# A hybrid decoder layer: weight sums of the seven-product pieces formed in earlier stages, kept in device memory, and used in every second piece

## The chip, the cores and the metric

The kernel runs on one core of one Trainium2 chip. Its time is the device time of one execution in microseconds, and lower is better. Five engines work side by side, each through its own list of instructions in a fixed order: PE (TensorE, matrix products), DVE (VectorE), ACT (ScalarE), POOL (GpSimd) and SP (SyncE, which here only issues transfers). Transfers issued by SP, ACT and POOL run on the core's 16 DMA engines. An instruction that has to wait holds up all that stand behind it on its engine.

## The reference

One layer of a decoder with 256 tokens and 16 meta tokens in front, width 2048, all in float32. What costs time are four weight matrices:

```python
h    = concat([meta, x])                                   # 272 x 2048
proj = rms_norm(h) @ w_in                                  # 2048 -> 12320
yA   = grouped_rms_norm(B * conv3(C * v))                  # short convolution, 16 groups
yB   = grouped_rms_norm(SSD(silu(conv4(xBC)), dt) * silu(z))   # state space, 8 groups
h    = h + rms_norm(concat([yA, yB]) @ w_out)              # 4096 -> 2048
h    = h + rms_norm(square(relu(rms_norm(h) @ w_ff1)) @ w_ff2)  # 2048 -> 8192 -> 2048
return h[16:]
```

Weights have 4 bytes each: 100 MB for `w_in`, 34 MB for `w_out`, 67 MB each for `w_ff1` and `w_ff2`. All are read once from device memory.

## The kernel before

**Three products for one.** TensorE multiplies in a format with fewer bits (float32r), so each operand is split into a high part (a rounded copy, made by ACT) and a low part (the difference, made by DVE). A product is then high x high + high x low + low x high: three matmuls.

**Pieces.** The weights come in 256 pieces of 1 MB, each 128 partitions x 2048 values: 96 of `w_in`, 32 of `w_out`, 64 of `w_ff1`, 64 of `w_ff2`. For a piece, SP loads `raw` (three buffers), ACT makes `wh` (three buffers), DVE makes `wl` (two or three), PE uses both. `load(i)` writes this down; the program asks for a piece two ahead of the one that PE works on. A raw buffer is free for the next load once `wl` has been made from it.

**Stages.** (1) Input projection: 24 groups of four pieces; activations are the moving operand, so the results stand feature by feature, and the convolutions, the state-space part and the group norms of earlier groups are worked in between by DVE, ACT and small matmuls. The first four pieces are loaded in 16 slices of 128 rows (`split_input`), each with one slice of the input. (2) Output projection and (4) second feed-forward product: `tok_stationary`. Here tokens are stationary, in two blocks of 128, the weights move 512 columns at a time, and the output is done in two halves of 1024 columns; a piece has two slices of 128 rows and 1024 columns. (3) First feed-forward product, 16 blocks of four pieces.

**The seven-product form.** A plain piece of stage 2 or 4 is a 2 x 2 block product (two token blocks, two slices of rows, two column blocks): eight block products, 24 matmuls of 512 columns. In some pieces the Strassen-Winograd form is used: seven block products, 21 matmuls, for which four sums of weights (`t`, then its parts `th`, `tl`) and four sums of activations (`js`, then `mix`) are needed. Some of the products go into a second set of four PSUM banks, `shared`, which is spread over the outputs once in each half (`spread_shared`, `shared_late`). Before the change 5 pieces of `w_out` and 14 of `w_ff2` (every fourth) take this form. Their sums are made shortly before use by `add_up` (L189 to L194): DVE subtracts 128 x 1024 and twice 128 x 512, ACT copies, DVE subtracts 128 x 2048.

**What sets the order.** The instructions are written in program order and then ordered for each engine, at build time, by a scheduler with a timeline of its own (`schedule_with_timeline_sim=True`); an instruction may be put ahead of others when its engine and its inputs are free in that timeline. The order doesn't change when the kernel runs. `later` and `pump` place small matmuls between the large ones.

In the profile of the kernel before, L175 makes `wl` in the projection and L174 its `wh`; L646 to L648 and L643 are the projection's matmuls; L1089 and L1090 those of the first feed-forward product; L791 to L793 those of plain pieces in `tok_stationary`, L822 to L824 of seven-product pieces. In the changed kernel lines are some 13 to 34 higher.

Of the kernel before, what the change touches and what calls it, by code (L numbers as in the profile page):

```python
# [9 lines left out]
F32 = mybir.dt.float32  # L10
# [36 lines left out]
def hymba_layer(ctx: ExitStack, tc: tile.TileContext, ht, x, meta, vec, cst, g1, g3,  # L47
# [14 lines left out]
    raws = ctx.enter_context(tc.tile_pool(name="raws", bufs=3, side="right"))  # L62
    yctx = ctx.enter_context(ExitStack())
# [116 lines left out]
    seven, sums = {}, {}  # L180

    def add_up(i):

        if i not in seven or i in sums:
            return
        raw = fetch(i, ("raw",))[0]
        rows_in(i, raw, slice(0, 2))
        t, th, tl = seven[i]()
        nc.vector.tensor_sub(t[:, 0:2], raw[:, :, 512:], raw[:, 0].rearrange("p (a n) -> p a n", a=2))  # L189
        nc.vector.tensor_sub(t[:, 2], raw[:, 1, 512:], t[:, 0])  # L190
        nc.vector.tensor_sub(t[:, 3], raw[:, 1, :512], t[:, 2])
        for half in (slice(0, 2), slice(2, 4)):
            nc.scalar.copy(th[:, half], t[:, half])
        nc.vector.tensor_sub(tl, t, th)  # L194
        sums[i] = (raw, th, tl)

    def load(i):
# [34 lines left out]
    cst_sb = const.tile([P, NCST], F32, name="cst_sb")  # L232
# [69 lines left out]
    with ExitStack() as p1:  # L302
# [24 lines left out]

        def split_input(k):
# [9 lines left out]
            if k == 8:  # L338
                nc.sync.dma_start(vec_sb[:, V_GCN:], vec[:, V_GCN:])
                nc.sync.dma_start(cst_sb, cst)  # L340
# [139 lines left out]
        def dt_consts():  # L480
            ts(vec_sb[:, V_CW:V_DSK], vec_sb[:, V_CW:V_DSK], 0.5, None, op0=ALU.mult)
            nc.vector.tensor_copy(nsel.rearrange("p i m -> p (i m)"), cst_sb[:, C_NS:C_NS + 384])
# [5 lines left out]
        pers = p1.enter_context(tc.tile_pool(name="pers", bufs=1))  # L488
        xem, bmt = [], []
# [165 lines left out]
        for gi, (kind, idx) in enumerate(groups):  # L655
# [12 lines left out]
            for j in range(4):  # L668
# [9 lines left out]
                wh, wl = parts[4 * gi + j]  # L678
                if gi == 4:
# [69 lines left out]
    def tok_stationary(base, korder, src, parity, dst, gain, ssq, r, tail, done, between, late=None, sixth=None,  # L749
                       fast=((), ()), mixp=None, half_gain=None):  # L750
# [7 lines left out]
        for h in range(2):  # L758
            for i in fast[h]:
                seven[base + npc * h + i] = room  # L760

        def prep(i):
# [10 lines left out]
            if base + i in seven:  # L773
                a11, a21, a12, a22 = (s[:, k, P * b:P * (b + 1)] for k in range(2) for b in range(2))
                a = left.tile([P, 4, P], F32, tag="junk", name="js")
                ah_, al_ = mixes()
# [18 lines left out]
        def mixes():  # L795
# [3 lines left out]
        def seven_products(d, x, h, i, first, last):  # L799
# [15 lines left out]
            def t(j):  # L815
                return th[:, j], tl[:, j]
# [353 lines left out]
```

## Time and profile before

| | |
|---|---|
| time, median of 3 runs | 1507.97 us (1507.62 to 1508.58) |
| the profiled execution | 1508.04 us, of which the span from the first to the last instruction is 1506.2 us |
| PE | 1490.7 us busy, 9187 matmuls |
| DVE | 1117.2 us busy, 1680 instructions |
| ACT | 839.4 us busy, 1303 instructions |
| POOL | 1.1 us busy, 8 instructions |
| DMA | 281.49 MB, 187 GB/s over the span |
| HBM | 277.90 MB read, 2.10 MB written |

In a profile row an instruction is named by line, engine, operation, and what it writes and reads (`wl<-raw,wh`), then the sizes. In rows in order of time the first number is the start in us, the second the duration; `x2` means that instructions in a row were put together. In rows by groups the numbers behind the bar are busy time in us, the mean of one in ns, and the idle time of the engine before them with what ended it. In rows of stretches there is the busy time of each engine with its number of instructions, then the clock granted to TensorE, the share of time that the DMA engines were busy, and their GB/s.

### The profile page before, as it was taken

The page shows a single profiled execution, that of the slowest core. Times are in us where ns is not written, and L with a number is a line of the kernel's source. Part 1 is how long each engine was busy: PE and PEld are TensorE (multiplying, and loading weights), DVE is VectorE, ACT ScalarE, POOL GpSimd, SP SyncE. Part 2 cuts the span into 40 slices and gives each one's busy share as a digit, 9 for nine tenths or more (in the row PEclk, how much of TensorE's full clock was granted, in tenths as well). Part 3 has the DMA queues.
Part 4 walks back from the last instruction along what each step waited for, and adds up shares of the span by engine and source line. Part 5 has one row for each costly group of instructions (what it writes and reads, how often), then busy time and mean ns, then how long its engine had stood idle before and what let it go on. Part 6 is the DMA issues. An engine that isn't in the chain of part 4 may idle for free.

```text
span 1506.2 us, 23037 instructions
## 1 busy us (share of the span) xinstructions
PE 1490.7 (99%) x9187; PEld 1337.3 (89%) x9187; DVE 1117.2 (74%) x1680; ACT 839.4 (56%) x1303; POOL 1.1 (0%) x8
## 2 busy tenths in 40 slices
PE   8999999999999999999999999999999999999997
PEld 8999899999999999988887888888888888888886
DVE  7698888667765776797878666666666788789776
ACT  6655555455544554556557655556556555556552
POOL 0000000000000000000000000000000000000000
PEclk9999999999999999999999999999999999999999
DMA  9665555556545646575664555565555656657562
GB/s 306 230 191 159 150 143 166 163 173 169 167 144 185 176 149 215 188 232 196 197 222 143 193 186 184 190 196 192 184 188 191 210 196 208 209 161 247 190 201 84
DMA packets 151676, 281.49 MB, mean 187 GB/s; under 512 B 8064, under 2 KB 59392, under 8 KB 150912
## 3 DMA queue, kind: packets, MB, share of 16 engines
q1 hardware_dynamic: 150848, 275.83, 57.1%
q10 hardware_dynamic: 720, 4.19, 0.7%
q8 instruction: 72, 1.18, 0.3%
q14 instruction: 36, 0.29, 0.1%
HBM read 277.90 MB, written 2.10 MB: 186 GB/s over the span
## 4 chain that ended last, share of the span: by engine, by line
PE 95%; DMA 2%; DVE 1%; ACT 1%; issue 0%; SPq 0%; DVEq 0%; ACTq 0%
PE mm L1089 15%; PE mm L648 11%; PE mm L647 10%; PE mm L646 10%; PE mm L791 9%; PE mm L792 9%; PE mm L793 9%; PE mm L1090 7%; PE mm L643 3%; PE mm L823 2%; PE mm L824 2%; PE mm L822 2%; DMA raw<-w_in 2%; PE aux L613 1%; PE mm L1007 1%; PE mm L1005 1%
## 5 line engine op out<-in xcount | busy, mean ns | idle before, releaser
L648 PE MATMUL mm<-XX,wl 128*128 128x256 f32 (+3 forms) x1536 | 427.2, 285 | 0.0
L646 PE MATMUL mm<-XX,wh 128*128 128x258 f32 (+3 forms) x1344 | 382.1, 288 | 5.4 <-ACT wh L174 5.4
L647 PE MATMUL mm<-XX,wh 128*128 128x258 f32 (+3 forms) x1344 | 379.3, 286 | 0.0
L1089 PE MATMUL mm<-h,wh 128*128 128x512 f32 x960 | 333.2, 394 | 0.0
L175 DVE TENSOR_TENSOR wl<-raw,wh 128x1024 fp32r<-128x1024 f32 (+1 forms) x223 | 256.0, 1182 | 99.5 <-PE mm L648 56.5
L174 ACT CAST wh<-raw 128x1024 fp32r<-128x1024 f32 (+1 forms) x223 | 218.0, 1017 | 164.8 <-PE mm L647 121.9
L648 PEld LDWEIGHTS mm<-XX,wl 128*128 128x128 f32 x1536 | 286.5, 189 | 1.4 <-issue 0.2
L1090 PE MATMUL mm<-h,wl 128*128 128x256 f32 x960 | 265.7, 277 | 0.0
L646 PEld LDWEIGHTS mm<-XX,wh 128*128 128x128 f32 x1344 | 253.1, 190 | 7.7 <-ACT wh L174 5.4
L647 PEld LDWEIGHTS mm<-XX,wh 128*128 128x128 f32 x1344 | 252.6, 189 | 1.5 <-issue 0.7
L216 DVE SCALAR_TENSOR_TENSOR wl<-raw,vec_sb,wh 128x512 fp32r<-128x512 f32 x256 | 175.5, 747 | 98.5 <-ACT wh L215 98.5
L792 PE MATMUL mm<-wl,jh 128*128 128x512 f32 x616 | 239.4, 389 | 0.0
L793 PE MATMUL mm<-wh,jl 128*128 128x512 f32 x616 | 239.0, 389 | 0.0
L791 PE MATMUL mm<-wh,jh 128*128 128x512 f32 x616 | 233.1, 390 | 0.0
L1089 PEld LDWEIGHTS mm<-h,wh 128*128 128x128 f32 x960 | 180.0, 188 | 41.5
L222 DVE TENSOR_TENSOR wl<-raw,wh 128x2048 fp32r<-128x2048 f32 x75 | 171.8, 2290 | 56.0 <-ACT wh L220 53.4
L215 ACT ACTIVATE wh<-raw,vec_sb 128x512 fp32r<-128x512 f32 x256 | 163.8, 712 | 87.0 <-PE mm L1089 50.5
L1090 PEld LDWEIGHTS mm<-h,wl 128*128 128x128 f32 x960 | 180.3, 188 | 0.3
L220 ACT CAST wh<-raw 128x1024 fp32r<-128x1024 f32 x150 | 149.5, 1045 | 39.6 <-PE mm L824 25.5
L792 PEld LDWEIGHTS mm<-wl,jh 128*128 128x128 f32 x616 | 115.6, 188 | 23.9
L793 PEld LDWEIGHTS mm<-wh,jl 128*128 128x128 f32 x616 | 115.6, 188 | 23.9
L791 PEld LDWEIGHTS mm<-wh,jh 128*128 128x128 f32 x616 | 115.6, 188 | 24.0
(610 smaller groups left out, 1470.4 us busy)
## 6 DMA issues: line engine op xcount, KB each, us to landing
raw<-w_ff SPq DMA_DIRECT2D x128, 1024.0 KB, 5.1
raw<-w_in SPq DMA_DIRECT2D x60, 1024.0 KB, 5.2
raw<-w_out SPq DMA_DIRECT2D x32, 1024.0 KB, 5.1
raw<-w_in SPq DMA_DIRECT2D x80, 256.0 KB, 4.8
raw<-w_in SPq DMA_DIRECT2D x32, 512.0 KB, 4.1
xn<-x SPq DMA_DIRECT2D x2, 1024.0 KB, 5.2
xt<-x ACTq DMA_DIRECT2D x2, 1024.0 KB, 6.3
out<-fg SPq DMA_DIRECT2D x8, 256.0 KB, 2.1
```

Source lines behind the costliest of these rows:

```text
L174: nc.scalar.copy(wh[:, ks], raw[:, ks])
L175: nc.vector.tensor_sub(wl[:, ks], raw[:, ks], wh[:, ks])
L216: stt(wl[:, k], raw[:, k], g, wh[:, k].bitcast(F32), op0=ALU.mult, op1=ALU.subtract)
L222: nc.vector.tensor_sub(wl, raw, wh)
L646: mm(o[:, :n], lhsT=wh[:, k, fs], rhs=XH[kk][:, lo:], start=(kk == 0), stop=False)
L647: mm(o[:, :n], lhsT=wh[:, k, fs], rhs=XL[kk][:, lo:], start=False, stop=False)
L648: mm(o[:, :n], lhsT=wl[:, k, fs], rhs=XH[kk][:, lo:], start=False, stop=last)
L791: mm(o, lhsT=yh[:, k, bs], rhs=wh[:, k, ns], start=first, stop=False)
L792: mm(o, lhsT=yh[:, k, bs], rhs=wl[:, k, ns], start=False, stop=False)
L793: mm(o, lhsT=yl[:, k, bs], rhs=wh[:, k, ns], start=False, stop=last)
L1089: mm(o, lhsT=wh[:, k, fs], rhs=both, start=(kk == 0), stop=False)
L1090: mm(o[:, :SEQ], lhsT=wl[:, k, fs], rhs=both[:, :SEQ], start=False, stop=(kk == KD - 1))
```

## The change

The pieces in the seven-product form become 9 of `w_out` (7, 9, 11, 13 of the first half, 2, 4, 6, 8, 10 of the second) and 27 of `w_ff2` (every second one). For each of these 36 pieces, `ahead` loads the whole piece by a transfer on POOL's queue into a tile `pre`, forms the four sums there in place by four DVE subtractions of 128 x 512 (L203, L204, L206, L207), and stores the tile to device memory, again on POOL's queue. In the program these steps stand in the projection from the ninth group on, one step for each piece, and in the first feed-forward product, three steps in each block; `pre` has two buffers there, and one here. In `tok_stationary` the finished sums are read back by SP (`ut`) and split into `th` and `tl`, in halves, after the fourth of the seven products of the piece before in that form; `ut`, `th` and `tl` have one buffer. Of the piece itself only three quarters are loaded again. The products are written in another order, those with sums first. Part of a constant table is loaded into a scratch tile, which frees the room.

```diff
+    OUT7 = [(7, 9, 11, 13), (2, 4, 6, 8, 10)]
+    FF7 = [range(2, 29, 2), range(2, 27, 2)]
...
+    seven, begun, pres, todo = set(order7), {}, [], list(order7)
+
+    def ahead(step):
+
+        if step == 0:
...
+            begun[i] = pres[-1].tile([P, 2048], F32, tag="pre", name="pre")
+            (_, _, src), = pieces[i][1]
+            nc.gpsimd.dma_start(begun[i].rearrange("p (k n) -> p k n", k=2), src)
+            begun["last"] = i
             return
...
+        w11, w12, w21, w22 = (begun[i][:, 512 * j:512 * (j + 1)] for j in range(4))
+        if step == 1:
+            nc.vector.tensor_sub(w11, w12, w11)
+            nc.vector.tensor_sub(w12, w22, w12)
+        else:
+            nc.vector.tensor_sub(w22, w22, w11)
+            nc.vector.tensor_sub(w21, w21, w22)
+            kept = dram.tile([P, 2048], F32, name=f"u{i}")
+            nc.gpsimd.dma_start(kept, begun[i])
+            begun[i], begun["last"] = kept, None
...
         if i in seven:
-            add_up(i)
-            raw, th, tl = sums[i]
-            wh, wl = fetch(i, ("wh", "wl"))
-            halve(raw, wh, wl, slice(1, 2))
-            nc.scalar.copy(wh[:, 0, :512], raw[:, 0, :512])
-            nc.vector.tensor_sub(wl[:, 0, :512], raw[:, 0, :512], wh[:, 0, :512])
+            tiles = [t.rearrange("p k n -> p (k n)")[:, :1536] for t in fetch(i)]
+            raw, wh, wl = tiles
+            (_, _, src), = pieces[i][1]
+            nc.sync.dma_start(raw[:, :512], src[:, 0, :512])
+            nc.sync.dma_start(raw[:, 512:], src[:, 1])
+            nc.scalar.copy(wh, raw)
+            nc.vector.tensor_sub(wl, raw, wh)
             parts[i] = (wh, wl)
             return
...
+        pres.append(p1.enter_context(tc.tile_pool(name="pre1", bufs=2, side="right")))
...
+                if gi >= 8:
+                    n = 4 * (gi - 8) + j
+                    if n < 63:
+                        ahead(n % 3)
...
+        def sums_in(n):
+            if n < len(line):
+                nc.sync.dma_start(ut, begun[base + line[n]])
+
+        def sums_split(n):
+            if n < len(line):
+                for half in (slice(0, 1024), slice(1024, 2048)):
+                    nc.scalar.copy(th[:, half], ut[:, half])
+                    nc.vector.tensor_sub(tl[:, half], ut[:, half], th[:, half])
+                sums_in(n + 1)
...
+                if j == 3:
+                    sums_split(line.index(npc * h + i) + 1)
                 pump()
...
-                add_up(base + npc * h + i + 3)
+                if npc * h + i == max(0, line[0] - 3):
+                    sums_in(0)
+                    sums_split(0)
...
+    pres.append(tctx.enter_context(tc.tile_pool(name="pre2", bufs=1, side="right")))
...
+            if j != 1:
+                ahead((0, 0, 1, 2)[j])
```

Where the scheduler put the new instructions is seen in the built order of three places. First POOL, from its last memsets on (`pre` is the tile, `u_...` the tile in device memory; the brackets name semaphores that are waited for, `DMASW` those of POOL's own transfers). Before, nothing stood behind the memsets.

```order
L513 MEMSET xem_149 128x256
L514 MEMSET bmt_150 128x128
L513 MEMSET xem_153 128x256
L514 MEMSET bmt_154 128x128
L195 DMA pre<-w_out 128x2x1024 x2
L209 DMA u_2840<-pre 128x2048 [waits DMASW0_49,DVE_49]
L209 DMA u_3117<-pre 128x2048 [waits DMASW1_49,DVE_49]
L195 DMA pre<-w_out 128x2x1024 [waits DMASW2_49]
L195 DMA pre<-w_out 128x2x1024 [waits DMASW3_49]
L209 DMA u_3360<-pre 128x2048 [waits DMASW4_49,DVE_49]
```

The first two loads wait for nothing, the next two only for the stores of the buffers.

Second, DVE's first instructions, before and now. L337 (now L355) makes the low part of a slice of the input, L175 (now L176) that of a slice of weights; names of tiles are two higher now.

```order
L337 SCALAR_TENSOR_TENSOR XX_112<-hs_134,vec_sb,XX_112 128x272
L175 TENSOR_TENSOR wl<-raw,wh 128x512
L337 SCALAR_TENSOR_TENSOR XX_113<-y_88,vec_sb,XX_113 128x272
L175 TENSOR_TENSOR wl<-raw,wh 128x512
L337 SCALAR_TENSOR_TENSOR XX_114<-y_89,vec_sb,XX_114 128x272
```

```order
L355 SCALAR_TENSOR_TENSOR XX_114<-hs_136,vec_sb,XX_114 128x272
L203 TENSOR_TENSOR pre<-pre 128x512
L204 TENSOR_TENSOR pre<-pre 128x512
L176 TENSOR_TENSOR wl<-raw,wh 128x512
L206 TENSOR_TENSOR pre<-pre 128x512
L355 SCALAR_TENSOR_TENSOR XX_115<-y_90,vec_sb,XX_115 128x272
L207 TENSOR_TENSOR pre<-pre 128x512
L203 TENSOR_TENSOR pre<-pre 128x512
L204 TENSOR_TENSOR pre<-pre 128x512
L176 TENSOR_TENSOR wl<-raw,wh 128x512
L206 TENSOR_TENSOR pre<-pre 128x512
L355 SCALAR_TENSOR_TENSOR XX_116<-y_91,vec_sb,XX_116 128x272
```

Two sets of subtractions now stand among the second, third and fourth slices of the start.

Third, DVE in the projection, in the stretch from 79 to 144 us of the profile before (the short convolution's `y` and the `dt_` chain of the state-space part), before and now.

```order
L175 TENSOR_TENSOR wl<-raw,wh 128x1024 x2
L719 TENSOR_TENSOR q<-cs_t,mm 128x258
L413 SCALAR_TENSOR_TENSOR dt_e<-dt_e,nr 32x272
L719 TENSOR_TENSOR q<-cs_t,mm 128x258
L413 SCALAR_TENSOR_TENSOR dt_e<-dt_e,nr 32x272
L722 SCALAR_TENSOR_TENSOR y_87<-q,vec_sb,y_87 128x256
```

```order
L176 TENSOR_TENSOR wl<-raw,wh 128x1024 x2
L747 SCALAR_TENSOR_TENSOR y_88<-q,vec_sb,y_88 128x256
L203 TENSOR_TENSOR pre<-pre 128x512
L746 SCALAR_TENSOR_TENSOR y_88<-q,vec_sb,y_88 128x256
L432 SCALAR_TENSOR_TENSOR dt_e<-dt_e,nr 32x272
L743 TENSOR_TENSOR q<-cs_t,mm 128x258
L204 TENSOR_TENSOR pre<-pre 128x512
L747 SCALAR_TENSOR_TENSOR y_88<-q,vec_sb,y_88 128x256
L432 SCALAR_TENSOR_TENSOR dt_e<-dt_e,nr 32x272
L206 TENSOR_TENSOR pre<-pre 128x512
```

A set is spread between the other work there. Counted over DVE's whole list, the 21 sets that the program puts into the projection from its 33rd piece on all stand before the low part of the 38th piece, and those in the first feed-forward product begin in the last part of the output projection.

More of the change, by code (lines that the diff above doesn't have):

```diff
@@ L175, in halve @@
         nc.vector.tensor_sub(wl[:, ks], raw[:, ks], wh[:, ks])
-    seven, sums = {}, {}
-    def add_up(i):
-        if i not in seven or i in sums:
-            return
[L186 to L195, printed above, removed]
+    OUT7 = [(7, 9, 11, 13), (2, 4, 6, 8, 10)]
+    FF7 = [range(2, 29, 2), range(2, 27, 2)]
+    order7 = [base + 32 // (2 if base == base_out else 1) * h + i
+              for base, sets in ((base_out, OUT7), (base_ff2, FF7)) for h in range(2) for i in sets[h]]
+    seven, begun, pres, todo = set(order7), {}, [], list(order7)
+    def ahead(step):
+        if step == 0:
+            if not todo:
+                return
+            i = todo.pop(0)
+            begun[i] = pres[-1].tile([P, 2048], F32, tag="pre", name="pre")
+            (_, _, src), = pieces[i][1]
+            nc.gpsimd.dma_start(begun[i].rearrange("p (k n) -> p k n", k=2), src)
+            begun["last"] = i
+            return
+        i = begun.get("last")
+        if i is None:
+            return
+        w11, w12, w21, w22 = (begun[i][:, 512 * j:512 * (j + 1)] for j in range(4))
[8 more added lines that the diff above has]
+            begun[i], begun["last"] = kept, None
     def load(i):
@@ L326, in hymba_layer @@
         rq = xp.tile([P, 3, 3], F32, name="rq")
+        ns_sb = scratch("sq")[:, :NCST - C_NS]
         def split_input(k):
@@ L841, in shared_late @@
         def shared_late(four):
-            _, hi, lo = room()
+            hi, lo = (e.rearrange("p (j n) -> p j n", j=4) for e in (th, tl))
             for j, blk in ((0, 0), (1, 1)):
@@ L919, in rstd, with room @@
         rsqrt(dst, *(rv[:, blk, i:i + 1] for i in range(3)), meanwhile)
-    def room(n=3):
-        return [h2p.tile([P, 2048], d, tag=f"h2{c}", name=n_).rearrange("p (k n) -> p k n", k=4)
-                for c, (n_, d) in enumerate((("t", F32), ("th", F32R), ("tl", F32R))[:n])]
-    def mixp():
-        return h2p.tile([P, 1024], F32R, tag="h23", name="mix")
+    def room():
+        ut, th, tl, mix = (h2p.tile([P, 2048], d, tag=f"h2{c}", name=n)
+                           for c, (n, d) in enumerate((("ut", F32), ("th", F32R), ("tl", F32R), ("mix", F32R))))
+        return ut, th, tl, mix.rearrange("p (s i k t) -> p s i k t", s=2, i=2, k=4)
     idr = left.tile([P, P], F32R, name="idr")
@@ L993, in hymba_layer @@
     tok_stationary(base_out, k_out, yt, 0, [hres[:, 0], hres[:, 1]], None, ssq[:, 0], rr[:, 0], TAIL,
-                   lambda blk: blk or residual(blk), between, late, first_gain, ((7, 10), (2, 6, 10)), mixp)
+                   lambda blk: blk or residual(blk), between, late, first_gain, OUT7)
     drain()
```

37 lines of the change are left out of this document (17 added, 20 removed).

## The prediction

> **What bounds the kernel now.** I read the page first, then the stretches, then single instructions at three places: the start, the input projection, and a piece in the seven-product form.
>
> ```profile
> PE 1490.7 (99%) x9187; PEld 1337.3 (89%) x9187; DVE 1117.2 (74%) x1680; ACT 839.4 (56%) x1303; POOL 1.1 (0%) x8
> DVE  7698888667765776797878666666666788789776
> DMA  9665555556545646575664555565555656657562
> PE 95%; DMA 2%; DVE 1%; ACT 1%; issue 0%; SPq 0%; DVEq 0%; ACTq 0%
> ```
>
> PE is busy for 99% of the span and makes up 95% of the chain that ended last. So a matmul that is taken away is worth its time, and everything else costs only where it makes PE wait. The slices of DVE and of the DMA engines are not even, though, and the averages (74% and 6 tenths) hide what matters for this change: where the new work is put. These are the stretches it falls into, and two where it does not:
>
> ```profile
> core 0: us, PE busy (x) PEld busy (x) DVE busy (x) ACT busy (x) POOL busy (x), PEclk, DMA share, GB/s
> 10.00:20.00 10.00, 10.00 (x85) 10.00 (x84) 9.77 (x25) 8.09 (x17) 0.00 (x0) 1.00 1.07 360
> 5.00:30.00 25.00, 24.57 (x189) 24.58 (x190) 20.70 (x44) 18.37 (x35) 0.00 (x0) 1.00 1.00 322
> 31.00:79.00 48.00, 47.47 (x392) 47.24 (x392) 31.16 (x52) 30.83 (x42) 0.00 (x0) 1.00 0.71 248
> 79.00:144.00 65.00, 65.00 (x537) 64.58 (x536) 60.08 (x121) 35.66 (x61) 0.00 (x0) 1.00 0.58 163
> 144.00:201.00 57.00, 57.00 (x404) 52.02 (x403) 45.36 (x81) 29.38 (x51) 0.00 (x0) 1.00 0.52 148
> 201.00:245.00 44.00, 44.00 (x355) 43.01 (x354) 40.44 (x73) 28.33 (x44) 0.00 (x0) 1.00 0.56 168
> 245.00:620.00 375.00, 375.00 (x2964) 364.39 (x2963) 259.10 (x402) 182.67 (x263) 0.00 (x0) 1.00 0.55 172
> 841.00:1150.00 309.00, 309.00 (x1785) 270.19 (x1784) 197.25 (x345) 182.85 (x341) 0.00 (x0) 1.00 0.59 194
> 1200.00:1300.00 100.00, 100.00 (x443) 82.84 (x442) 80.88 (x84) 57.95 (x72) 0.00 (x0) 1.00 0.62 201
> ```
>
> From 5 to 30 us the DMA engines have no room at all (share 1.00). From 79 to 245 us DVE has little: 4.92, 11.64 and 3.56 us idle in the three stretches. From 245 us on it has room (116 us idle before 620).
>
> **What the change takes away.** Each piece that goes from four products to seven products saves 24 - 21 = 3 matmuls of 512 columns. Their pace stands in the second feed-forward stage, in a piece that already has the form:
>
> ```profile
> 1200.42 0.39 PE L822 MATMUL mm<-wh,jh 128*128 128x512 f32 x1
> 1204.95 0.39 PE L824 MATMUL mm<-th,jl 128*128 128x512 f32 x1
> 1205.18 0.39 PE L791 MATMUL mm<-wh,jh 128*128 128x512 f32 x1
> ```
>
> The 21 matmuls of this piece start from 1200.42 on, the next piece at 1205.18: 4.76 us, or 0.2267 us each. The form goes from 19 pieces (5 and 14) to 36 (9 and 27): 17 x 3 x 0.2267 = **-11.56 us**. The additions that gather the shared parts exist in each half already, so nothing is added there.
>
> **Can those two stages bear it?** A pair of pieces (one plain, one seven) then lasts 24 x 0.2267 + 4.76 = 10.20 us.
>
> ```profile
> L222 DVE TENSOR_TENSOR wl<-raw,wh 128x2048 fp32r<-128x2048 f32 x75 | 171.8, 2290 | 56.0 <-ACT wh L220 53.4
> L771 DVE TENSOR_TENSOR jl<-h,jh 128x512 fp32r<-128x512 f32 x64 | 44.0, 688 | 19.4 <-ACT jh L770 19.2
> L782 DVE TENSOR_TENSOR mix<-js,mix 128x512 fp32r<-128x512 f32 x19 | 13.0, 685 | 0.0
> L193 ACT CAST th<-t 128x1024 fp32r<-128x1024 f32 x38 | 39.6, 1049 | 5.3 <-DVE t L189 3.4 <-issue 1.4 <-DVE t L191 0.5
> raw<-w_ff SPq DMA_DIRECT2D x128, 1024.0 KB, 5.1
> ```
>
> DVE has in a pair: 2.29 (plain low part), about 1.8 (low part of 1536 columns, between 0.69 and 2.29), about 2.4 (low part of the sums, two halves, 2.29 in one piece), 2 x 0.69, 0.69, and four small ones that I put at 0.3 each: 9.8, with starts a little closer than durations, so it fits into 10.20, barely. The single tile of split sums is free after the fourth product, 2.7 us into a seven piece, and wanted again at 10.2: 7.5 us for two ScalarE copies and two DVE subtractions of half a tile, in a chain 2 x 1.05 and half of 2.29, some 3.3 us. The read-back must land in one period (10.2 us against 5.1). DMA: 1 + 0.75 + 1 MB in 10.2 us is 283 GB/s against 360 seen above. I take **0**; were DVE 1 us over in every pair, it would be 36 x 1 us.
>
> **What it adds, and where.** 36 loads and 36 stores of 1 MB on POOL's queue, 36 read-backs on SP's (less a quarter of those 36 weights), and 36 sets of four DVE subtractions of 128x512. For 19 pieces that DVE work existed in the later stages; now all is ahead. Price of a set:
>
> ```profile
> L190 DVE TENSOR_TENSOR t<-raw,t 128x512 f32<-128x512 f32 x19 | 13.0, 684 | 0.0
> 1209.15 0.69 DVE L190 TENSOR_TENSOR t<-raw,t 128x512 f32<-128x512 f32 x1
> 1209.75 0.69 DVE L771 TENSOR_TENSOR jl<-h,jh 128x512 fp32r<-128x512 f32 x1
> ```
>
> Starts are 0.60 us apart in a row: 4 x 0.60 + 0.05 = 2.45 us. The source asks for the sets from the ninth group of the projection on. The built order says otherwise: nothing on POOL's queue keeps the first loads back, so they stand at the kernel's very start, two sets stand among DVE's first twenty rows, and all 21 sets of the projection stand before the low part of its 38th piece (of 96), which DVE now finishes at 245 us. The other 15 lie between the end of the output projection and the last third of the first feed-forward stage.
>
> *Start: +10 us (5.8 to 17.5).* Now:
>
> ```profile
> 1.38 0.20 POOL L494 MEMSET bmt<- 128x128 f32 x1
> 8.86 0.69 DVE L175 TENSOR_TENSOR wl<-raw,wh 128x512 fp32r<-128x512 f32 x1 [0.58 <-ACT wh L174]
> DMA packets 7850, 8.75 MB, mean 292 GB/s; under 512 B 2768, under 2 KB 4944, under 8 KB 7848
> 20.57 7.27 DMA raw<-w_in
> 27.94 1.06 ACT wh L174
> 29.02 0.99 DVE wl L175
> 30.16 1.22 DVE wl L175
> 30.45 0.29 PE L646 MATMUL mm<-XX,wh 128*128 128x258 f32 x1
> ```
>
> SP's 8.75 MB of the first 30 us fill the DMA engines, and they have no slack at the end: the fifth piece's low part is done (30.0 for its first half) just as PE begins that piece (30.45). POOL is free at 1.58. Its two first loads (2.10 MB) then share the engines with SP; DVE stops at the first set until the first load has landed, and again until the second has, with the low part of the third slice (8.86 now) behind that; then both stores follow (2.10 MB more). 4.19 MB at 360 GB/s are 11.6 us by which SP's bytes come later. Lower bound: the two loads alone, 5.8 us. Upper: the next two loads get in as well, 6.29 MB, 17.5 us. I take 10, near the four transfers, since part of the second store may fall behind. The Trainium skill (DMA: Bandwidth & Descriptors, Queues, rings and completion order) says that each DMA engine takes turns, packet by packet, between the queues that have work; by that POOL's transfers are served at once, as I assume. If they stood behind SP's instead, this term would be 0 and the sum 1510.5; no run shown here has two full queues side by side.
>
> *Projection, 31 to 245 us: +11 us (0 to 25).* By the order, sets 3 to 7 stand in the stretch 31:79, 8 to 12 in 79:144, 13 to 18 in 144:201, 19 to 21 in 201:245. Against DVE's idle time there: 12.2 against 16.8 (fits), 12.2 against 4.9 (7.3 over), 14.7 against 11.6 (3.1 over), 7.4 against 3.6 (3.8 over): 14.2 us too late at the end. PE notices what exceeds the lead that the low parts have:
>
> ```profile
> 91.61 2.35 DVE L175 TENSOR_TENSOR wl<-raw,wh 128x1024 fp32r<-128x1024 f32 x2
> 93.45 0.28 PE L646 MATMUL mm<-XX,wh 128*128 128x256 f32 x1
> 151.62 2.35 DVE L175 TENSOR_TENSOR wl<-raw,wh 128x1024 fp32r<-128x1024 f32 x2
> 159.07 0.40 PE L643 MATMUL mm<-XX,wh 128*128 128x512 f32 x1
> ```
>
> It is nothing at one piece (done 93.96, begun 93.45) and 5.1 us at another (153.97, 159.07). Less a lead of some 3 us: 11. Lower bound 0, if ScalarE's and PE's waits move along and all idle time between 31 and 245 (37 us against 46.6) and the lead cover it; upper 25, if half of that idle time can't be used because DVE waits there for something else. DMA in this stretch: a set per 11.3 us is 2.10 MB, 186 GB/s beside 163 to 168: about 350, close to full, with two buffers. I put its own share at 0 here and leave it to a rival.
>
> *Between output projection and feed-forward: +3 us (0 to 8).* There is one buffer now. DVE stops at the second set until its load has landed, and that load waits for the first set's store: two transfers of 5.1 us with some ten short DVE instructions and four of 0.6 between; behind it on DVE stand the sums of squares and the residual on which the next stage waits. 10.2 us against some 7 us of such work (by 0.6 for each of 512 columns and 0.2 for a short one): about 3 are uncovered.
>
> *First feed-forward stage: 0 (0 to 12).*
>
> ```profile
> 1000.25 0.41 DVE L1047 TENSOR_TENSOR t__10418<-t__10418,mm 128x256 f32<-128x256 f32 x1
> 1022.44 0.41 DVE L1047 TENSOR_TENSOR t__10618<-t__10618,mm 128x256 f32<-128x256 f32 x1
> ```
>
> Four pieces take 22.19 us, DVE is idle for 112 of 309 us, so 15 sets (37 us) fit. Each set waits for store and load in turn through one buffer; in the later part sets stand 3.2 pieces (17.9 us) apart. With 2.45 to 5 us of subtractions and twice 5.1 to 7 that just goes round.
>
> **Sum.** 1508.04 (this execution; the median is 1507.97, the span 1506.2) - 11.56 + 10 + 11 + 3 + 0 = **1520.5 us**, slower by 0.8%.
>
> **Rivals.**
> *All of the saving arrives.* DVE's average is 74%, DMA's 58%, POOL's 0%, and idle slots take the sets: 1496.5, with up to 4 us of start left 1497 to 1501. It needs the start and projection terms together under 8 us. For it: 37 us of idle DVE time before 245, and a lead of 3 to 5 us at most pieces. Against it: a share of 1.00 and more up to 30 us, where PE begins a piece within half a microsecond of its weights. Chance 0.13.
> *POOL's round trip sets the pace.* 1 MB against SP's stream takes 8 rather than 5.1 us, so a round in the single buffer is 4 + 16 = 20 against 17.9, nine times over 2.1 us is 19, less a lead of 7: +12; in the projection two buffers, each round 24 us for 22.6 available, cost some 10 more than the DVE term. 1530 to 1545. For it: 350 of 360 GB/s; against it: DVE's catching up after 245. Chance 0.20.
> *The terms cancel:* losses of 9 to 14 give 1505 to 1511. Chance 0.05.
> *It does not do what it says:* the order has 51 matmuls fewer on PE, so this is out.
>
> **How the numbers follow.** Forecast 0.62, around it 1512 to 1530. A measurement of this kernel can tell 0.2%, 3 us, from no change. Faster 0.13, same 0.05, slower 0.82. Eight in ten: from 1500 (most of the first rival left out) to 1542.
>
> **What will show it.** Right: POOL loads landing 7 us or more after issue within the first 20 us; DVE idle before the first subtraction of sets 1 and 2, on a DMA; the fifth piece on PE at 38 to 45 us instead of 30.45; PE idle on DVE's low parts between 79 and 245; the projection's end some 20 us later; the second feed-forward stage shorter by 9 us with no idle PE. Wrong: the fifth piece still at 31 to 34 us, PE idle of a few us in the projection, or PE waiting for split sums in the last stage, which I put at nothing.

## The result, and the profile after

The changed kernel takes 1557.66 us (median of 4 runs, 1555.92 to 1560.53) against 1507.80 us of the kernel before: a ratio of 1.0328 (95% interval 1.0315 to 1.0341). It is slower, as forecast, but by 49.9 us where 12.4 were forecast, and outside the range that ended at 1542. The profiled execution took 1555.92 us with a span of 1554.1.

From the page of the changed kernel (lines from L175 on stand some 13 to 34 lower than in the kernel before):

```profile
PE 1501.4 (97%) x9136; PEld 1344.7 (87%) x9136; DVE 1214.3 (78%) x1886; ACT 870.6 (56%) x1318; POOL 46.8 (3%) x80
PEclk8999999999999999999999999999999999999999
DMA  9988899656645564677776798787866788868882
PE 79%; DMA 9%; DVE 7%; ACT 3%; issue 2%; SPq 1%; DVEq 0%; POOL 0%; ACTq 0%; POOLq 0%
```

PE has the 51 matmuls fewer that the change promises (9136 against 9187), and yet 10.7 us more of busy time, and its share of the chain that ended last fell from 95% to 79%. The slices say where to look: the DMA engines are near full for seven slices (272 us) and at some 4 to 6 tenths in the nine after them, and the clock granted to PE is below full in the first slice. PE's first matmuls of the ninth and the 49th piece of the input projection (each piece has 16 first products, so these are the 129th and the 769th), first in the kernel before, then in the changed one, with the fifth piece too:

```profile
55.38 0.37 PE L646 MATMUL mm<-XX,wh 128*128 128x258 f32 x1
317.58 0.39 PE L643 MATMUL mm<-XX,wh 128*128 128x512 f32 x1
```

```profile
46.40 0.39 PE L666 MATMUL mm<-XX,wh 128*128 128x258 f32 x1 [2.00 <-ACT wh L175]
84.58 0.40 PE L666 MATMUL mm<-XX,wh 128*128 128x258 f32 x1
367.86 0.39 PE L663 MATMUL mm<-XX,wh 128*128 128x512 f32 x1
```

29.2 us are lost by the ninth piece, 50.3 by the 49th, and not one more until the projection ends. Counted in the same way, by the first or the last matmul of a stage, the table says how late the profiled execution of each run of this study is against that of the kernel before (us, negative is earlier; e3 to e6, e10 and e11 are one execution each). The out projection should gain 2.7 us (4 x 3 x 0.2267) and the second feed-forward stage 8.8 (13 x 3 x 0.2267).

| kernel | 9th piece | 49th piece | projection ends | first ff stage begins | second ff stage begins | last matmul |
|---|---|---|---|---|---|---|
| changed | 29.2 | 50.3 | 50.3 | 55.0 | 56.3 | 47.4 |
| e1 all loads held, projection | -0.7 | 2.7 | 23.4 | 28.9 | 29.3 | 20.4 |
| e2 all loads held, both | 0.2 | 4.8 | 24.3 | 21.6 | 38.7 | 30.5 |
| e3 first two held, to 33rd piece | 0.9 | 7.0 | 9.4 | 13.8 | 14.2 | 5.4 |
| e4 first two held, to 57 us | 1.5 | 38.5 | 38.5 | 42.9 | 44.0 | 35.2 |
| e5 quarter transfers | 6.4 | 31.1 | 31.1 | 36.8 | 57.4 | 48.6 |
| e6 short subtractions | 30.8 | 30.9 | 30.9 | 30.2 | 45.5 | 36.7 |
| e7 sets pinned, projection | 0.0 | 0.0 | -0.1 | 7.6 | 7.9 | -1.0 |
| e8 sets pinned, both | 0.0 | -0.1 | -0.1 | 0.6 | 0.6 | -8.3 |
| e9 pinned, four pieces earlier | 1.0 | 0.8 | 1.1 | -1.5 | -1.5 | -10.4 |
| e10 two loads at the start | 8.6 | 8.9 | 8.8 | 9.1 | 9.1 | 0.2 |
| e11 two sets at the start | 16.9 | 19.3 | 19.2 | 19.3 | 19.3 | 10.4 |

So the changed kernel's account is 29.2 (to the ninth piece) + 21.1 (from there to the 49th) + 7.4 (between the projection's end and the feed-forward stage: 55.0 - 50.3 + 2.7) + 1.3 (in that stage) - 11.6 (saved) = 47.4 us at the last matmul. The saving came in full: 56.3 - 47.4 = 8.9 in the last stage.

**The start.** The queues of the DMA engines up to the ninth piece, in the kernel before (55 us) and in the changed one (85 us); columns are packets, MB, share:

```profile
q1 hardware_dynamic: 10912, 16.41, 89.7%
```

```profile
q1 hardware_dynamic: 11362, 17.01, 58.7%
q0 software_dynamic: 2349, 11.54, 35.7%
```

SP's queue (q1) moves its 16 to 17 MB in both; POOL's (q0) puts 11.54 MB beside them: six loads and five of the stores that answer them, where I had counted two and two. POOL's issues in the timeline show it (start, duration, what ended the idle time before):

```profile
1.53 1.55 POOL L195 DMA_DIRECT2D pre<-w_out  x2
14.64 0.57 POOL L209 DMA_DIRECT2D u<-pre  x1 [11.56 <-DVE pre L207]
22.10 0.72 POOL L195 DMA_DIRECT2D pre<-w_out  x1 [2.77 <-DMA u<-pre]
26.95 0.73 POOL L195 DMA_DIRECT2D pre<-w_out  x1 [4.12 <-DMA u<-pre]
57.62 0.71 POOL L195 DMA_DIRECT2D pre<-w_out  x1
61.93 0.73 POOL L195 DMA_DIRECT2D pre<-w_out  x1 [3.60 <-DMA u<-pre]
```

Two pieces of the chain that ended last show what it cost (start, duration):

```profile
24.31 11.84 DMA raw<-w_in
62.27 10.22 DMA xn<-x
```

Both are loads of SP's, of weights and of the input whose norms PE needs ahead of the ninth piece; the second kind took 4.0 to 5.6 us in the kernel before. PE's waits between 5 and 85 us name the same two places (us in total, times, longest):

```profile
PE mm L666 <- ACT wh L175: 15.3, 7, 6.2
PE aux L383 <- DVE dg L382: 7.5, 1, 7.5
```

Of the 15.3 us, 6.2 lie before PE's first matmul of all, where the kernel before has 5.4; the other six waits make 9.1. PE begins the eighth piece 17.6 us late (first row before, second row changed), so 11.6 of the 29.2 us come between it and the ninth, where the fifth and sixth load stand beside `xn<-x` and PE waits for the norms (L383):

```profile
47.41 0.28 PE L646 MATMUL mm<-XX,wh 128*128 128x258 f32 x1
```

```profile
65.02 0.28 PE L666 MATMUL mm<-XX,wh 128*128 128x258 f32 x1
```

**The stretch after it.** Stretches up to 84 us, from 84 to 300 us and two of 4 us in the changed kernel, then two of the kernel before (columns: the stretch and its length, busy time of PE, PEld, DVE, ACT and POOL with instructions, granted clock, DMA share, GB/s):

```profile
0.00:84.00 84.00, 60.25 (x407) 57.84 (x408) 49.88 (x92) 39.72 (x63) 8.24 (x19) 0.86 0.95 337
84.00:300.00 216.00, 203.22 (x1509) 194.41 (x1508) 198.91 (x365) 106.74 (x174) 19.66 (x31) 0.96 0.87 295
20.00:24.00 4.00, 4.00 (x36) 4.00 (x36) 3.05 (x6) 1.65 (x3) 0.72 (x1) 1.00 1.04 393
32.00:36.00 4.00, 3.41 (x17) 3.12 (x15) 1.19 (x2) 1.14 (x2) 0.00 (x0) 0.50 1.03 378
```

```profile
0.00:55.00 55.00, 49.05 (x389) 48.81 (x390) 32.96 (x68) 37.83 (x61) 1.05 (x8) 1.00 0.90 300
84.00:300.00 216.00, 216.00 (x1704) 208.63 (x1703) 178.60 (x321) 114.72 (x187) 0.00 (x0) 1.00 0.54 158
```

From 84 to 300 us two things rose at once, DVE from 178.6 to 198.9 us of 216 and the DMA engines from 0.54 to 0.87; this row cannot say which of the two PE waits for. That is for the experiments. DVE's instructions themselves are not slower beside POOL's transfers: a low part of 1024 columns takes 1.21 us on average between 84 and 300 us, and 1.22 in the kernel before between 55 and 250.

### The profile page after: what moved, and what is told of

Same layout as the page of the kernel before. It is cut to its first block, busy times and chain, and to the rows that moved or that the text cites. A ratio compares the mean times of both kernels' runs of the same rounds, so it can differ in the third digit from the quotient of the medians.

```text
span 1554.1 us, 23570 instructions
## 1 busy us (share of the span) xinstructions
PE 1501.4 (97%) x9136; PEld 1344.7 (87%) x9136; DVE 1214.3 (78%) x1886; ACT 870.6 (56%) x1318; POOL 46.8 (3%) x80
## 4 chain that ended last, share of the span: by engine, by line
PE 79%; DMA 9%; DVE 7%; ACT 3%; issue 2%; SPq 1%; DVEq 0%; POOL 0%; ACTq 0%; POOLq 0%
PE mm L1123 11%; PE mm L668 10%; PE mm L666 8%; PE mm L667 8%; PE mm L825 6%; PE mm L826 6%; PE mm L827 6%; PE mm L1124 6%; PE mm L851 3%; PE mm L852 3%; PE mm L853 3%; PE mm L663 3%; DMA raw<-w_in 3%; DMA pre<-w_ff 3%; DVE wl L176 2%
## 5 line engine op out<-in xcount | busy, mean ns | idle before, releaser
L666 PE MATMUL mm<-XX,wh 128*128 128x258 f32 (+3 forms) x1344 | 383.4, 293 | 24.3 <-ACT wh L175 15.3
L176 DVE TENSOR_TENSOR wl<-raw,wh 128x1024 fp32r<-128x1024 f32 (+1 forms) x204 | 232.7, 1177 | 86.2 <-PE mm L668 39.8
L175 ACT CAST wh<-raw 128x1024 fp32r<-128x1024 f32 (+1 forms) x204 | 197.8, 1013 | 179.9 <-PE mm L667 108.4
L826 PE MATMUL mm<-wl,jh 128*128 128x512 f32 x480 | 186.6, 390 | 0.0
L827 PE MATMUL mm<-wh,jl 128*128 128x512 f32 x480 | 186.1, 390 | 0.0
L825 PE MATMUL mm<-wh,jh 128*128 128x512 f32 x480 | 184.3, 391 | 0.0
L238 DVE TENSOR_TENSOR wl<-raw,wh 128x2048 fp32r<-128x2048 f32 x58 | 132.8, 2290 | 17.9 <-ACT wh L236 17.8
L236 ACT CAST wh<-raw 128x1024 fp32r<-128x1024 f32 x116 | 115.6, 1045 | 11.7 <-DMA raw<-w_out 6.0
L827 PEld LDWEIGHTS mm<-wh,jl 128*128 128x128 f32 x480 | 90.2, 188 | 19.0
L826 PEld LDWEIGHTS mm<-wl,jh 128*128 128x128 f32 x480 | 90.4, 188 | 18.6
L825 PEld LDWEIGHTS mm<-wh,jh 128*128 128x128 f32 x480 | 90.3, 188 | 18.6
```

The lines of the kernel that those rows point to most:

```text
L175: nc.scalar.copy(wh[:, ks], raw[:, ks])
L176: nc.vector.tensor_sub(wl[:, ks], raw[:, ks], wh[:, ks])
L666: mm(o[:, :n], lhsT=wh[:, k, fs], rhs=XH[kk][:, lo:], start=(kk == 0), stop=False)
L825: mm(o, lhsT=yh[:, k, bs], rhs=wh[:, k, ns], start=first, stop=False)
L826: mm(o, lhsT=yh[:, k, bs], rhs=wl[:, k, ns], start=False, stop=False)
L827: mm(o, lhsT=yl[:, k, bs], rhs=wh[:, k, ns], start=False, stop=last)
```

## The experiments

Two theories run through them: theory A is that the losses come from the place where the sets stand, B that each set costs its DVE time wherever it stands.

**e1 and e2: hold every load.** A copy of one column on POOL reads the low part of the current piece and writes into the tile to be loaded, so the load cannot start before it.

```diff
             (_, _, src), = pieces[i][1]
+            if held is not None:
+                nc.gpsimd.tensor_copy(begun[i][:, :1], held[:, 0, :1].bitcast(F32))
             nc.gpsimd.dma_start(begun[i].rearrange("p (k n) -> p k n", k=2), src)
...
-                        ahead(n % 3)
+                        ahead(n % 3, wl)
```

> Every load of a set in the projection is held on POOL by a copy of one column that reads the low part of the piece beside which the source names it (every third piece from the 33rd on); the 15 sets of the feed-forward stage stay as they are. Theory A (the place: the first 11.5 MB of POOL's transfers fall into the 84 us in which SP's stream fills the DMA engines, and the sets after them into the stretch up to 300 us in which DVE has no room): the 29.2 us lost by the ninth piece and the 21.1 us lost from there to the 49th both go, the 53 us of the transition and the saving stay: 1557.7 - 50.3 = 1507.4, say 1503 to 1510, and the 49th piece begins on PE at 317 to 321 us as in the kernel before (367.9 in the changed one). Theory B (the price of a set: 50.3 us over 21 sets are 2.4 us, just its four subtractions of 0.6, so a set costs PE its DVE time wherever it stands): the losses move with the sets behind the 33rd piece, and the time stays at 1550 to 1558.

Measured: 1529.35 us, ratio 1.0142 (1.0121 to 1.0163). Neither theory had it. The start is whole again and the 49th piece is 2.7 us late, as A says, but the projection then loses 21 us more, which A does not. DVE's waits between 230 and 660 us name a new cause:

```profile
DVE pre L205 <- DMA pre<-w_ff: 30.5, 8, 6.2
DVE pre L205 <- issue: 19.8, 7, 4.1
DVE pre L205 <- DMA pre<-w_out: 13.2, 5, 3.9
```

L205 is a set's first subtraction. The order on DVE is fixed when the program is built. The load is now issued late, and DVE stops at the set until it has landed, with the next low parts behind it. That the builder's timeline took the load to be sooner is my reading of it.

e2 holds the loads of the feed-forward stage in the same way (`ahead((0, 0, 1, 2)[j], wl)`).

> As the run with the projection's loads held, and the 15 loads of the feed-forward stage are held in the same way on the low part of the piece where the source names them. Theory A: the 7.4 us lost between the output projection and the feed-forward stage and the 1.3 us inside it go too: 1497 to 1500, faster than the kernel before by 0.5 to 0.7%. Theory B: as much as the run before it, 1550 to 1558. If a set is paced only by its single buffer in that stage (load, subtractions, store in turn), the transition's 7.4 us move into the stage: 1505 to 1508.

Measured: 1534.14 us, ratio 1.0176 (1.0150 to 1.0201): wrong for all three cases. The table splits it: between the projection's end and the feed-forward stage it gains 2.7 us (24.3 to 21.6), so the 7.4 us lost there are gone, as A says; but the stage itself now loses 17.1 us, with DVE stopped at the first subtraction for a load again (10 times, 59.4 us in all, 8.9 at the longest, put down to the load).

**e3 and e4: hold only the first two loads**, on the 33rd and 36th piece's low part (e3), or on the norms' broadcast `R0`, which stood at 57.6 us before (e4). All later loads follow as POOL's queue and the two buffers allow.

```diff
-                        ahead(n % 3)
+                        ahead(n % 3, wl if n < 6 else None)            (e3)
+                        ahead(n % 3, R0[:, :1] if n < 6 else None)     (e4)
```

> Only the first two loads of the projection are held, on the low part of the 33rd and 36th piece; all behind them run as fast as POOL's queue, the two buffers and DVE let them. Theory A (place alone): from 245 us on DVE was idle for 116 of 375 us and the DMA engines at 0.55, so 21 sets fit: as with all loads held, 1503 to 1512. Theory C (pace: sets that run without a pause take the DMA engines to 0.9 and DVE to full wherever they stand, as they did between 84 and 300 us at 21.1 us): 1507 + 21 = 1528, say 1520 to 1533. Theory B: 1550 to 1558.

> Only the first two loads are held, on the norms' broadcast that stood at 57.6 us in the kernel before, so that no transfer of POOL falls into the first 55 us; all behind them run freely from there. Theory A: the ninth piece begins at 55 to 58 us (84.6 in the changed kernel, 55.4 in the kernel before): the start's 29.2 us go. The sets then meet the stretch 60 to 300 us with six more of them to do there, so its 21.1 us stay or grow to 30: 1557.7 - 29.2 = 1528.5, up to 1538. Theory D (one late start: the late start itself throws later work against the sets, and the second loss hangs on the first): both go, 1507 to 1512. Theory B: 1550 to 1558.

e3: 1513.84 us, 2 us above A's range and clearly neither B nor C: sets that run without a pause cost 9.4 us in the projection there, with this row between 245 and 460 us:

```profile
245.00:460.00 215.00, 211.89 (x1657) 203.76 (x1658) 186.24 (x305) 99.88 (x148) 20.90 (x33) 0.99 0.92 314
```

The DMA engines are as full here (0.92) as in the changed kernel's bad stretch (0.87), and PE stands still for 3 us, not 13. e4: 1543.70 us. The start's 29.2 us are gone (1.5 left), as A says; but 37.0 us are lost from the ninth to the 49th piece, more than the 21.1 to 30 that I gave, so the time is 5.7 us above A's range. Theories B and D are out: D wanted both losses gone. All 21 sets now fall there, not 15. Six more sets are 14.7 us of DVE time (6 x 2.45), and the loss grew by 15.9: in that stretch a set more costs about its whole DVE time.

**e5 and e6: bytes or DVE.** e5 moves a quarter of each piece and subtracts as much as before; e6 moves everything and subtracts 8 of 512 columns.

```diff
-            nc.gpsimd.dma_start(begun[i].rearrange("p (k n) -> p k n", k=2), src)
+            nc.gpsimd.dma_start(begun[i][:, :512], src[:, 0, :512])
...
-            nc.gpsimd.dma_start(kept, begun[i])
+            nc.gpsimd.dma_start(kept[:, :512], begun[i][:, :512])       (e5)
...
-        w11, w12, w21, w22 = (begun[i][:, 512 * j:512 * (j + 1)] for j in range(4))
+        w11, w12, w21, w22 = (begun[i][:, 512 * j:512 * (j + 1)] for j in range(1) for _ in range(4))     (e5)
...
-                nc.sync.dma_start(ut, begun[base + line[n]])
+                nc.sync.dma_start(ut.rearrange("p (k n) -> p k n", k=2), pieces[base + line[n]][1][0][2])     (e5)
...
-        w11, w12, w21, w22 = (begun[i][:, 512 * j:512 * (j + 1)] for j in range(4))
+        w11, w12, w21, w22 = (begun[i][:, 512 * j:512 * j + 8] for j in range(4))     (e6)
```

> The changed kernel with POOL's loads and stores of a quarter of each piece (256 KB in place of 1 MB), the four subtractions of each set at full size on that quarter; the read-back takes the weights themselves, so the gathered sums are left out of the result. What is lost by the ninth piece (29.2 us) and from there to the 49th (21.1 us): Theory G (bytes at the start, DVE after it): a quarter of 11.5 MB at 345 GB/s is 8 us, so 3 to 9 us by the ninth piece, and 8 to 21 us from there to the 49th, since DVE's share of the work is the same. Rival H (bytes in both): 3 to 9 us and under 6 us. Rival I (DVE in both: the sets stand ahead of the first low parts): 20 us or more by the ninth piece.

> The changed kernel with all its transfers and the four subtractions of each set on 8 of 512 columns each (most of the sums is left out, so the result is not the reference's). Theory G: 25 to 30 us by the ninth piece, as with the whole subtractions, and under 8 us from there to the 49th, because DVE has its 2.45 us a set back. Rival H (bytes in both): 25 to 30 us and 15 us or more. Rival I (DVE in both): under 8 us and under 8 us.

Both leave part of the sums out of the result. In all, e5 takes 1557.09 us and e6 1545.16; what counts is where they lose. The first matmul of the ninth and of the 49th piece in e5, and its stretch from 84 to 300 us:

```profile
61.81 0.37 PE L666 MATMUL mm<-XX,wh 128*128 128x258 f32 x1
348.69 0.39 PE L663 MATMUL mm<-XX,wh 128*128 128x512 f32 x1
```

```profile
84.00:300.00 216.00, 199.68 (x1484) 188.75 (x1483) 197.11 (x363) 103.79 (x174) 14.68 (x27) 0.97 0.58 174
```

The same of e6:

```profile
86.18 0.28 PE L666 MATMUL mm<-XX,wh 128*128 128x258 f32 x1
348.47 0.39 PE L663 MATMUL mm<-XX,wh 128*128 128x512 f32 x1
```

```profile
84.00:300.00 216.00, 214.62 (x1675) 206.06 (x1673) 187.49 (x396) 116.92 (x192) 18.44 (x29) 1.00 0.92 310
```

The two losses come apart. With a quarter of the bytes the start loses 6.4 us (29.2 before), and the stretch after it 24.7, though the DMA engines are at 0.58 there. With short subtractions the start loses 30.8 us, and the stretch after it 0.1, though the DMA engines are at 0.92. Theory G holds on both sides (e5's 24.7 are 4 above its 21, e6's 30.8 are 0.8 above its 30): bytes at the start, DVE behind it. H and I are out. In e5 the sets also come round faster, the last one is done at 220 us and not at 297, which may be why it loses more there than the changed kernel; e6's 15 sets stand where the changed kernel's do (101 to 297 us there, 104 to 288 in e6).

Both lose much in the first feed-forward stage (20.6 and 15.3 us, where the changed kernel loses 1.3), which I had not expected. In e6 DVE stops there for loads 12 times, 68.2 us in all: the same waits as in e2. Why the changed kernel, with 27.9 us of such waits in six places, loses almost nothing was not tried separately.

**e7 and e8: loads early, subtractions late.** Only the first two loads are held (as in e3), and each set's subtractions are tied in DVE's own order behind the newest low part at the place where the source names them. The loads are then free to run up to two sets ahead.

```diff
+        behind = tc.issue_after(begun["dve"].ins) if i in order7[:21] else nullcontext()      (e7: the projection)
+        behind = tc.issue_after(begun["dve"].ins) if True else nullcontext()                  (e8: both stages)
         if step == 1:
-            nc.vector.tensor_sub(w11, w12, w11)
-            nc.vector.tensor_sub(w12, w22, w12)
+            with behind:
+                nc.vector.tensor_sub(w11, w12, w11)
+                nc.vector.tensor_sub(w12, w22, w12)
...                                                     (and the other two in the same way)
-        nc.vector.tensor_sub(wl[:, ks], raw[:, ks], wh[:, ks])
+        begun["dve"] = nc.vector.tensor_sub(wl[:, ks], raw[:, ks], wh[:, ks])
...
-                stt(wl[:, k], raw[:, k], g, wh[:, k].bitcast(F32), op0=ALU.mult, op1=ALU.subtract)
+                begun["dve"] = stt(wl[:, k], raw[:, k], g, wh[:, k].bitcast(F32), op0=ALU.mult, op1=ALU.subtract)      (e8)
```

> As the run with the first two loads held late, and each set's subtractions in the projection stand in DVE's order behind the newest low part at the place where the source names them, three pieces apart; the loads are free to run two sets ahead. Theory E (late loads: what the run with all loads held lost in the projection, 23.4 us, is DVE stopped at the first subtraction of a set, 43.7 us of waiting put down to the load and 19.8 us more at the same instruction, because the load had only just been issued): here DVE finds its load landed, the projection loses 0 to 4 us, the 7.1 us of the transition stay: 1507.7 - 11.6 + 2 + 7.1 = 1505, say 1503 to 1509. Rival F (each set's 2.45 us of DVE time make a low part late, wherever it stands): the 9.4 us of the run with the first two loads held stay: 1512 to 1516.

Measured: 1508.23 us, ratio 1.0001 (0.9992 to 1.0010). E is right about the projection, which loses nothing (-0.1), with all 21 sets and all their bytes in it; its row:

```profile
245.00:622.00 377.00, 377.00 (x2983) 366.54 (x2982) 304.00 (x489) 183.21 (x265) 23.93 (x38) 1.00 0.80 272
```

B and F are out. What is left is the step to the feed-forward stage, 7.7 us late plus 2.7 not gained, 3 us more than I gave.

> As the run before, and the sets of the feed-forward stage too stand behind the newest low part of the place where the source names them, four pieces apart, so that none stands in the transition. Theory A with E: the transition's 7 us go as well and nothing takes their place in the stage, where four pieces last 22 us against some 12 for a load and a store in the single buffer: 1496 to 1500, 0.5 to 0.8% faster than the kernel before. Rival: the single buffer or the first load behind the transition holds DVE in the stage as in the run with both held (17 us lost there): 1505 to 1515.

Measured: 1500.20 us, ratio 0.9949 (0.9936 to 0.9963): faster than both kernels, 0.2 us above what A with E gives. PE's wait at the step to the feed-forward stage in the changed kernel, DVE's stop there 6 us ahead of the residual (L993), and PE's wait in e8:

```profile
PE mm L1002 <- DVE hres L993: 6.6, 2, 6.4
```

```profile
838.93 0.69 DVE L203 TENSOR_TENSOR pre<-pre 128x512 f32<-128x512 f32 x1 [3.57 <-DMA pre<-w_ff]
```

```profile
PE mm L1007 <- DVE hres L998: 0.6, 1, 0.6
```

The stage itself loses 0.0. The 3.3 us missing lie between the projection's end (622.3 us) and the feed-forward stage; from 620 us on PE waits 1.7 us for a low part, 1.1 for the squares of a norm and these 0.6. The last of the 21 sets is done at 621 us, just ahead of them, which makes it the suspect that e9 tries.

**e9: four pieces earlier.**

```diff
-                if gi >= 8:
-                    n = 4 * (gi - 8) + j
+                if gi >= 7:
+                    n = 4 * (gi - 7) + j
```

> As the run with the sets of both stages pinned, the projection's sets named beside the 29th to the 89th piece in place of the 33rd to the 93rd, four pieces earlier, so that the last two no longer stand where the output projection begins (there the run before lost 3.3 us of its saving: 0.6 us late at its end where 2.7 should have been saved). If that loss is the last sets' DVE time and transfers: 3.3 us less, 1496 to 1498, and the output projection ends 2.7 us earlier than in the kernel before. If DVE between 212 and 242 us has no room for the two sets that now stand there (7.4 us busy too many in the forecast's count): what is won there is lost before the 37th piece: 1499 to 1503.

Measured: 1497.08 us (median of 5), ratio 0.9926 (0.9913 to 0.9940), the best of all; from the projection's end to the feed-forward stage it gains 2.7 us, as the first case says. Its page:

```profile
PE 1478.9 (99%) x9136; PEld 1326.6 (89%) x9136; DVE 1212.0 (81%) x1886; ACT 868.0 (58%) x1318; POOL 49.1 (3%) x82
```

As many matmuls as in the changed kernel, as much DVE work (1212.0 against 1214.3 us) and the same 385 MB, in 58 us less of span.

**e10 and e11: what a byte costs at the start.** e8 without the hold (two loads early, no store until the 36th piece), and with the first two sets formed at once.

```diff
-                        ahead(n % 3, wl if n < 6 else None)
+                        ahead(n % 3, None)                                              (e10, e11)
-        behind = tc.issue_after(begun["dve"].ins) if True else nullcontext()
+        behind = tc.issue_after(begun["dve"].ins) if i in order7[2:] else nullcontext() (e11)
```

> As the run with the sets of both stages pinned, with nothing to hold the first two loads: 2.10 MB of POOL's loads at the kernel's start and no store until the 36th piece. The changed kernel lost 29.2 us by the ninth piece with 11.5 MB. Theory G (the bytes, at the 337 GB/s that the DMA engines reached there): between 0 (16.4 MB of SP's and 2.1 at 337 GB/s are 55 us) and 2.10/337 = 6.2 us. Rival J (the order at the start: a load in SP's way makes the whole chain late, however few bytes): 12 us or more.

> As the run before, and the first two sets are free to be formed at once, as the changed kernel does: two loads, two stores and then the next two loads, 6.29 MB, all others pinned late. This is the upper bound of the forecast's start term (17.5 us). Theory G: (16.4 + 6.3)/337 is 67 us against 55, so 12 us, up to 6.29/337 = 18.7 us, by the ninth piece. Rival K (the forecast's price of a byte was too low: the 29 us come from the first two sets): 25 us or more. Rival I (DVE's place in line): 5 us or fewer.

POOL's queue up to the ninth piece, e10 and e11:

```profile
q0 software_dynamic: 544, 2.10, 8.6%
```

```profile
q0 software_dynamic: 1376, 6.29, 22.3%
```

2.10 MB cost 8.6 to 8.9 us (1508.98 us in all), 6.29 MB cost 16.9 by the ninth piece and 19.3 a little later (1518.95 us); the changed kernel's 11.54 MB cost 29.2. By the ninth piece e11 is inside G's range (12 to 18.7), and K and I are out. e11 is 16.6 us late at the eighth piece already and hardly later at the ninth, so the first 6.29 MB account for most of what the changed kernel loses up to the eighth (17.6), and the rest of its 29.2 comes with the transfers behind them. e10 lies between G's upper end (6.2) and J's lower (12): two loads alone cost more than their time on the engines. The first of them lands at 9.9 us, while SP's second slice of weights, which landed at 6.5 us before, now lands at 11.4; the second piece is already 5.7 us late. How much of the 8.9 us is order and how much bytes is open.

## Why the prediction was wrong

**Direction and saving: right.** 11.56 us were forecast to be saved and 11.6 were; the two stages that use the new form bear it without a wait of PE. Nothing in them waits for split sums, which I had listed as a way to be wrong.

**Start, +10 (5.8 to 17.5): the failing step, 29.2 measured.** It is 19.2 of the 35.0 us that the terms miss. The mechanism was right: the transfers at the kernel's start push SP's loads back, POOL is served at once, and the fifth piece begins at 46.40, just past the 38 to 45 forecast. The Trainium skill (DMA: Bandwidth & Descriptors, Queues, rings and completion order) says that an engine takes turns between the queues that have work. This trace agrees: the first set's first subtraction stands at 10.04, its load landed, while SP's slices of weights and input are still coming in (DMA share 0.94 from 4 to 10 us).

```profile
10.04 0.69 DVE L203 TENSOR_TENSOR pre<-pre 128x512 f32<-128x512 f32 x1 [0.45 <-DMA pre<-w_out]
```

The price was near too: two sets and the next two loads, 6.29 MB, cost 16.9 to 19.3 us in e11 where the upper bound said 17.5. What was wrong is the count. I stopped the sum at the fifth piece with two sets, because the order put only these among DVE's first rows. But the row from 31 to 79 us, with its DMA share of 0.71, has room for only (1 - 0.71) x 48 x 0.36 MB, about 5 MB (0.36 MB per us from the 360 GB/s row). By my own list sets 3 to 7 stand in that stretch, 10.5 MB, and I charged their DVE time there and none of their bytes.

**Projection, +11 (0 to 25): right mechanism, mis-sized, 21.1.** e6 shows that it is DVE alone: without the subtractions' length 0.1 us are lost, at a DMA share of 0.92. So putting the DMA's own share at 0 there was right. I let the sets fill all of DVE's gaps and then took a lead of 3 off. In the changed kernel 15 sets, 36.8 us, fell into the stretch and 21.1 came out as delay; in e4 21 sets, 51.5 us, and 37.0. Some 15 us were hidden in each. The same pieces lie between 55 and 250 us of the kernel before, and for e4 between 57 and 305, where DVE was idle for 23.7 and for 42.9 us:

```profile
55.00:250.00 195.00, 195.00 (x1532) 188.60 (x1531) 171.29 (x314) 110.08 (x180) 0.00 (x0) 1.00 0.56 165
57.00:305.00 248.00, 248.00 (x1969) 240.63 (x1969) 205.08 (x366) 131.81 (x210) 0.00 (x0) 1.00 0.54 162
```

So two thirds of the idle time hid work in the one and a third in the other; neither all of it, as I had it, nor a fixed half, as my upper bound of 25 had it. What I had summed was PE's waiting, and that was 12.8 us in the changed kernel (216.00 - 203.22), near my 11; that so much of the method was right may be luck, since in e4 PE waited 23.5 us between 84 and 300. The rest of the 21.1 is, by the account at the end of this section, the slower clock.

**Between the stages, +3 (0 to 8): 7.4, within its bounds.** DVE stopped for the load with the residual behind it, as written; e8 takes the sets away from there and 0.6 us of PE's wait remain. **First feed-forward stage, 0 (0 to 12): 1.3.**

**The rivals.** That POOL's round trip sets the pace has no support as it was put (e6: full transfers, 0.1 us lost from the ninth piece to the projection's end). It does hold where a load is issued late: in e1 and e2 DVE stood at the first subtraction for some 60 us, and 17 to 23 us reached PE. That all of the saving arrives (1497 to 1501) is what e8 and e9 reach, by moving the same work: it was a question of place, not of capacity.

**What no step had: the clock.** Idle time of PE is not all that its waits cost. Up to 84 us PE stood idle 23.75 us, against 5.95 us in the kernel before up to 55 us, so 17.8 more; and the granted clock over 84 us was 0.86, which is worth at most another 0.14 x 84 = 11.8: 29.6 together, where 29.2 were lost. It is at most that, because the clock was low in idle time too (0.50 from 76 to 80 us, PE busy for 1.17 of the 4); counted on PE's busy time alone, in stretches of 4 to 6 us, it is some 8.5. From 84 to 300 us 12.8 us idle and 0.04 x 216 = 8.6 make 21.4, the 21.1 that were lost. The two short stretches above show it in the small: 36 matmuls in 4 us at 20 us, 17 at 32 us, where the clock was 0.50. By this account some 17 to 20 of the 50 us are the slower clock behind the waits. It is an account from the rows; no run separated it. I had counted stalls at their own length.

The Trainium skill (TensorE: Matmul & The Clock Gate, HAM oscillation — how this bites in real kernels) puts its rule at idle gaps of PE above about 3.4 us. The trace agrees for the wait of 7.5 us, but not for that length as a limit: between 84 and 300 us no wait of PE is longer than 2.81 us, and four times the clock goes to 0.50 behind waits of 1.79 to 2.81. One of them, the wait and the clock just behind it:

```profile
135.13 0.36 PE L666 MATMUL mm<-XX,wh 128*128 128x272 f32 x1 [2.40 <-DVE y L754]
136.10:139.40 3.30, 3.30 (x17) 3.30 (x16) 3.30 (x5) 2.41 (x3) 0.00 (x0) 0.50 0.73 192
```

It does not follow every such wait: in e1 PE waits 2.60 us at 241 us and the clock stays at 1.00 up to 250. What decides is open here.

## What to carry to other kernels

Work that is moved off a busy stage must be given a place, not only a queue: on an idle queue whose loads wait for nothing it runs at once, at the kernel's start, where bytes are dearest. Check each stretch in which it lands against both resources, bytes and the in-order engine, and do not count all of an engine's idle time as usable where it waits for others (here a third to two thirds hid work). Issue the load well ahead and tie the dependent work behind something on its own engine; the same 36 sets then cost about 1 us of the 11.6 saved (e9 1497.08 us, the changed kernel 1557.66).

## What the runs showed of the hardware that was not expected

- A DMA share of 0.92 (310 GB/s) beside SP's stream cost PE 0.1 us from the ninth to the 49th piece (e6), while a share of 0.95 (337 GB/s) in the first 84 us went with 29.2 us lost. That the stream has a lead in the first case and none in the second is the likely reason; no run tried it.
- A load in competition lands late enough to matter: `xn<-x` 10.22 us in place of 4.0 to 5.6.
- Waits of 1.79 to 2.81 us were followed by a granted clock of 0.50 for 3.3 us and more, and by the account above each us that PE waited in the first 300 us went with another 0.56 to 0.67 us of slower clock (17.1 to 20.4 us to 30.6 us of waits).
